# S5 scan of a Hyena/S5 diffusion trunk: groups of channels paired on the 128 rows, turns and lag matrices laid out in DRAM beforehand

## The chip, the cores and the metric

The kernel runs on one core of a Trainium2 chip. The metric is the device time of one execution in microseconds (us), lower is better. All data are float32; most large products are three-pass products of rounded halves, the products of the S5 stage are plain float32.

## The reference, cut to what matters

The program is one denoising step of a trunk of two layers over 1024 latent and 256 context tokens of width 1024: Hyena mixer, SwiGLU, S5 mixer, SwiGLU, final norm. The change concerns the S5 mixer: 64 groups of 16 channels, 64 complex states each, scanned forward and backward.

```python
def _s5_scan(ug, ab_re, ab_im, bb_re, bb_im, init):
    bu_re = jnp.einsum('blgh,gph->blgp', ug, bb_re)
    bu_im = jnp.einsum('blgh,gph->blgp', ug, bb_im)
    ...
    pr, pi, hr, hi = lax.associative_scan(_cmul_combine, (a_re, a_im, bu_re, bu_im), axis=1)
    if init is not None:
        hr = hr + pr * h0r - pi * h0i
        hi = hi + pr * h0i + pi * h0r
    return hr, hi

def _s5_mixer(u, j, p, h0):
    y = uf * p['s5_D'][j]
    for d in range(2):
        src = ug if d == 0 else jnp.flip(ug, axis=1)
        hr, hi = _s5_scan(src, ab_re, ab_im, bb_re, bb_im, init)
        yd = einsum('ghp,blgp->blgh', C_re, hr) - einsum('ghp,blgp->blgh', C_im, hi)
        ...
        y = y + yd
        if h0 is None:
            finals.append(jnp.stack([hr[:, -1], hi[:, -1]], axis=1))
    y = jax.nn.gelu(y)
    a, g = jnp.split(y @ p['s5_glu_w'][j] + p['s5_glu_b'][j], 2, axis=-1)
    return a * jax.nn.sigmoid(g), fin
```

## The kernel before, in words

The stages follow each other: filters, Hyena projection, Hyena core, Hyena output, the first SwiGLU, the S5 stage, its gate (GLU), the second SwiGLU, the final norm. Two pieces of S5 preparation are coroutines run beside other stages. `s5_tables` runs beside the Hyena projection: it makes the turn factors `W` by repeated complex products (`cmul`, L1015 to L1020) and stores them as `K.rot` (L1177). `s5_matrices` runs beside the first SwiGLU: it makes the entering matrices `K.tin`, the leaving matrices `K.wout` (L1239) and the lag blocks `K.kd` (L1252). `S5Scan.begin` is called in the last step of that SwiGLU, and `S5Scan.run` is the S5 stage.

The tokens are cut into chunks of 8 steps, so a group has WG = 162 columns: a zero column, 128 latent chunks, another zero column, and 32 context chunks. The 64 groups are taken in 8 pieces `k` of 8 groups. A tile of states has 128 rows, 64 states of the forward direction over 64 of the backward one, and 8 x 162 = 1296 columns.

For one piece: `norm` makes the modulated input `h` (on VectorE at L1328, for pieces 4, 5 and 6 on GpSimd at L1326; ScalarE adds the bias at L1330) and eight DMAs from ScalarE's queue spread it over rows as `u` (L1333). `enter` multiplies `u` by `ti` (16 matmuls of 162 columns, L1352) into six PSUM tiles, and VectorE turns these by `T` (L1353 to L1356, twelve operations). `T` holds 128 columns per group from DRAM (L1293, two DMAs); its 32 context columns are copied by ScalarE (L1342, L1343). `entered` adds the crossed products on GpSimd (L1361, L1362) and ScalarE puts the cached state into the zero columns (L1364, L1365). `scan` fills the decay tile `D0` on ScalarE (L1372) and runs four scans on VectorE: forward on rows 0 to 63 (L1376), backward on rows 64 to 127 (L1377), each for the real and the imaginary part, with 1296 columns. ScalarE saves the final states (L1378, L1379). The result is turned back: two products on GpSimd (`c`, `d`, L1383, L1384), two on VectorE (L1385, L1386). `scanned` subtracts `c` on VectorE (L1389). `leave` loads `wo` and, by eight DMAs from `K.kd`, the lag matrices `it`; 32 matmuls (L1405) add four terms into three PSUM tiles, ScalarE applies gelu (L1408) and stores (L1409).

The loop over `k` runs, in this order, enter(k), scanned(k-2), entered(k), leave(k-2), scan(k-1), norm(k+2). It only gives the program order; a planning scheduler with modelled costs sets the final order on each engine, and each engine runs its own list strictly in that order.

Of the kernel before, what the change touches and what calls it, by code (L numbers as in the profile page):

```python
# [1022 lines left out]
def s5_tables(K, io):  # L1023
# [13 lines left out]
    with ExitStack() as c:  # L1037
# [99 lines left out]
        for k in range(8):  # L1137
# [30 lines left out]
            W = bp.tile([128, 2, 8, 128], F32, tag="W", name="W")  # L1168
            t = [bp.tile([128, 8, 32], F32, tag=f"t{i}", name="t") for i in range(2)]
            V.tensor_copy(out=W[:, :, :, 0], in_=b0[:, :, g])  # L1170
            for i in range(7):
                n = 1 << i
                for a in range(0, n, 32):
                    e = min(n, 32)
                    cmul(V, pair(W[:, :, :, n + a:n + a + e]), pair(W[:, :, :, a:a + e]),
                         pair(pu[:, i, :, g].unsqueeze(3).to_broadcast([128, 2, 8, e])), [x[:, :, :e] for x in t])
            nc.sync.dma_start(out=K.rot[k], in_=W)  # L1177
# [3 lines left out]
def s5_matrices(K, io, p):  # L1181

    nc = K.nc
# [26 lines left out]
    for q in range(16):  # L1210
# [28 lines left out]
        nc.sync.dma_start(out=K.wout[k][:, :, e * 4:e * 4 + 4], in_=To.rearrange("p r g j h -> p r g (j h)"))  # L1239
# [20 lines left out]

class S5Scan:

# [4 lines left out]
    def begin(self, c):  # L1267
# [6 lines left out]
        self.z = z = zp.tile([128, 2, 8 * WG + 2], F32, name="Z")  # L1274
        self.D0 = zp.tile([128, 8, WG], F32, name="D0")
        for t in T:
            V.memset(t[:, :, :, 0:130:129], 0.0)
        for k in range(3):
            self.turn(k)
        V.memset(z[0:64, :, 0:2], 0.0)  # L1280
        V.memset(z[64:128, :, 8 * WG:8 * WG + 2], 0.0)
        V.memset(self.D0[:, :, 0:130:129], 0.0)
        self.fin = zp.tile([128, 2, 64], F32, name="fin")
        self.hin = zp.tile([128, 2, 64], F32, name="hin")
        self.q = [zp.tile([128, 2, 64], F32, name=f"q{i}") for i in range(2)]
# [3 lines left out]
        cmul(V, pair(self.hin), pair(self.q[0]), pair(K.u8), self.tiny)  # L1289

    def turn(self, k):
        for ri in range(2):
            self.K.nc.sync.dma_start(out=self.T[k % 3][:, ri, :, 1:129], in_=self.K.rot[k][:, ri])  # L1293

    def run(self, outs):
# [8 lines left out]
        with ExitStack() as c:  # L1304
            tp = c.enter_context(tc.tile_pool(name="st", bufs=6, reuse_waits="tile"))
            up = c.enter_context(tc.tile_pool(name="su", bufs=3, reuse_waits="tile"))
            U, R, AB, CD, DU = {}, {}, {}, {}, {}
# [4 lines left out]
            def norm(k):  # L1312
# [19 lines left out]
                for j in range(8):  # L1332
                    DU[k] = S_.dma_start(out=u[j * 16:j * 16 + 16], in_=h[:, j])  # L1333

            def enter(k):
# [6 lines left out]
                S_.copy(t[0:64, :, :, 130:162], t[0:64, :, :, 1:33])  # L1342
                S_.copy(t[64:128, :, :, 130:162], t[64:128, :, :, 97:129])  # L1343
# [15 lines left out]
            def entered(k):  # L1359
# [3 lines left out]
                g = slice(k * 8, k * 8 + 8)  # L1363
# [365 lines left out]
```

## Time and profile before

| | |
|---|---|
| median of 3 runs | 3635.53 us (3634.86 to 3645.38) |
| profiled execution, its own time | 3644.13 us |
| its span, first to last instruction | 3642.4 us |
| TensorE busy | 3308.8 us, 91% of the span |
| VectorE busy | 2371.9 us, 65% |
| ScalarE busy | 967.2 us, 27% |
| GpSimd busy | 688.5 us, 19% |
| mean granted TensorE clock | 0.953 of full speed |

The shares are means over stages with different limits, and the S5 stage is 7% of the span. In the profile's names PE is TensorE, DVE VectorE, ACT ScalarE, POOL GpSimd, SP the queue of SyncE; PEld is TensorE's weight load; a q behind an engine (ACTq) is its DMA issue.

### The profile page before, as it was taken

Reading aid. Unit: us, or ns where it says so; the run is one execution under the profiler, and the core shown is the slowest. Engines: PE = TensorE matmul, PEld = TensorE weight load, DVE = VectorE, ACT = ScalarE, POOL = GpSimd, SP = SyncE. Lnnn points to the kernel's source line nnn. Section 1 sums busy time; section 2 is a strip of 40 time slices with the busy share of each in tenths; the row PEclk is TensorE's granted clock in tenths of the full one; section 3 lists DMA queues with packets and bytes.
Section 4 is the critical chain, followed back from the end, with each engine's and each line's share of the span. In section 5 each row is a group of like instructions: output and inputs, shape, how many; then the busy total and the mean of one; then the engine's idle time right before and its main releaser. Section 6 shows DMA issues by size and latency. Waiting matters only on the chain. (4 is left out here: it accounts for less than half of the span.)

```text
span 3642.4 us, 48098 instructions
## 1 busy us (share of the span) xinstructions
PE 3308.8 (91%) x19078; PEld 2834.9 (78%) x19078; DVE 2371.9 (65%) x3910; ACT 967.2 (27%) x1674; POOL 688.5 (19%) x670
## 2 busy tenths in 40 slices
PE   5899699998869999999999994559999999999997
PEld 3788588887757788888888884547878888888886
DVE  5888988869994655655665558994255454554546
ACT  3555433332224411111111131213151111111112
POOL 1212300000022344333341014740120000000002
PEclk8999799999979999999999997779999999999998
DMA  7776353465436122121111125734101111111101
GB/s 229 242 254 204 120 179 127 151 221 199 148 127 202 38 68 70 64 70 64 64 62 54 41 57 136 168 87 128 47 24 42 40 35 41 35 45 37 35 30 58
DMA packets 292439, 368.21 MB, mean 101 GB/s; under 512 B 38415, under 2 KB 230615, under 8 KB 283256
## 3 DMA queue, kind: packets, MB, share of 16 engines
q1 hardware_dynamic: 278392, 343.53, 29.2%
q10 hardware_dynamic: 11520, 11.15, 1.4%
q0 software_dynamic: 2304, 10.49, 0.9%
q8 instruction: 150, 2.46, 0.3%
q14 instruction: 73, 0.60, 0.1%
HBM read 268.49 MB, written 91.29 MB: 99 GB/s over the span
## 5 line engine op out<-in xcount | busy, mean ns | idle before, releaser
L36 PE MATMUL ps<-hh,hi 128*128 128x512 f32 (+1 forms) x2688 | 952.7, 358 | 14.2 <-ACT hh L225 10.3
L37 PE MATMUL ps<-hl,hi 128*128 128x512 f32 (+1 forms) x2688 | 957.9, 357 | 8.3 <-POOL hl L96 5.7
L38 PE MATMUL ps<-hh,lo 128*128 128x512 f32 (+1 forms) x2688 | 953.1, 355 | 0.0
L184 DVE SCALAR_TENSOR_TENSOR x<-ps,mod,x 128x512 f32<-128x512 f32 (+1 forms) x1056 | 629.9, 653 | 11.6 <-PE ps L38 11.6
L36 PEld LDWEIGHTS ps<-hh,hi 128*128 128x128 f32 x2688 | 506.5, 189 | 94.9 <-ACT hh L225 11.6
L167 DVE TENSOR_TENSOR nw<-nw,ps 128x512 f32<-128x512 f32 x132 | 78.8, 597 | 766.4 <-PE ps L38 760.9
L37 PEld LDWEIGHTS ps<-hl,hi 128*128 128x128 f32 x2688 | 508.9, 189 | 86.8 <-POOL hl L96 11.7
L38 PEld LDWEIGHTS ps<-hh,lo 128*128 128x128 f32 x2688 | 507.6, 189 | 73.6 <-issue 0.5
L37 PE MATMUL ps<-gl,hi 128*128 128x512 f32 (+1 forms) x1056 | 375.3, 355 | 0.0
L36 PE MATMUL ps<-gh,hi 128*128 128x512 f32 (+1 forms) x1056 | 373.4, 355 | 1.2 <-DVE x L184 1.2
L38 PE MATMUL ps<-gh,lo 128*128 128x512 f32 (+1 forms) x1056 | 374.2, 354 | 0.0
L57 POOL TENSOR_TENSOR st<-st,sq 128x512 f32<-128x512 f32 (+1 forms) x72 | 92.2, 1283 | 1180.2 <-ACT sq L56 1177.7
L32 DVE TENSOR_TENSOR lo<-raw,hi 128x1024 fp32r<-128x1024 f32 x156 | 207.0, 1327 | 94.9 <-ACT hi L31 94.6
L31 ACT CAST hi<-raw 128x1024 fp32r<-128x1024 f32 x156 | 163.6, 1049 | 350.9 <-PE ps L37 320.1
L36 PEld LDWEIGHTS ps<-gh,hi 128*128 128x128 f32 x1056 | 198.8, 188 | 32.0 <-DVE x L184 2.1
L37 PEld LDWEIGHTS ps<-gl,hi 128*128 128x128 f32 x1056 | 199.0, 188 | 29.4 <-issue 1.2
L38 PEld LDWEIGHTS ps<-gh,lo 128*128 128x128 f32 x1056 | 199.0, 188 | 28.8 <-issue 0.7
L36 PE MATMUL ps<-hh,wh 128*128 128x512 f32 (+1 forms) x576 | 210.3, 366 | 11.5 <-ACT hh L95 11.5
L37 PE MATMUL ps<-hl,wh 128*128 128x512 f32 (+1 forms) x576 | 208.6, 363 | 7.9 <-DVE hl L92 6.2
L38 PE MATMUL ps<-hh,wl 128*128 128x512 f32 (+1 forms) x576 | 207.5, 362 | 0.0
L170 ACT CAST gh<-nw 128x512 fp32r<-128x512 f32 x132 | 72.2, 547 | 483.7 <-DVE nw L167 483.7
L166 ACT ACTIVATE nw<-ps 128x512 f32<-128x512 f32 x132 | 69.3, 525 | 490.8 <-PE ps L38 489.7
(364 smaller groups left out, 5294.8 us busy)
## 6 DMA issues: line engine op xcount, KB each, us to landing
adaw<-in_ada_w SPq DMA_DIRECT2D x96, 512.0 KB, 5.0
raw<-in_w13p SPq DMA_DIRECT2D x88, 512.0 KB, 3.6
raw<-in_w2p SPq DMA_DIRECT2D x44, 512.0 KB, 3.2
kspec<-KO SPq DMA_DIRECT2D x16, 1024.0 KB, 5.1
K<-kspec SPq DMA_DIRECT2D x16, 1024.0 KB, 5.7
raw<-in_hy_inp SPq DMA_DIRECT2D x24, 512.0 KB, 3.3
rot<-W SPq DMA_DIRECT2D x8, 1024.0 KB, 6.9
tin<-tst SPq DMA_DIRECT2D x32, 256.0 KB, 2.7
```

Source lines behind the costliest of these rows:

```text
L31: K.nc.scalar.copy(hi, raw)
L32: K.nc.vector.tensor_tensor(out=lo, in0=raw, in1=hi.bitcast(F32), op=ALU.subtract)
L36: nc.tensor.matmul(ps, wh, xh, start=first, stop=False, **kw)
L37: nc.tensor.matmul(ps, wh, xl, start=False, stop=False, **kw)
L38: nc.tensor.matmul(ps, wl, xh, start=False, stop=last, **kw)
L57: nc.gpsimd.tensor_tensor(out=st, in0=st, in1=sq, op=ALU.add)
L166: nc.scalar.activation(out=sa, in_=ps[0], func=AF.Silu)
L167: nc.vector.tensor_tensor(out=sa, in0=sa, in1=ps[1], op=ALU.mult)
L170: nc.scalar.copy(gh, sa)
L184: K.nc.vector.scalar_tensor_tensor(out=x, in0=p, scalar=self.G(d, COND[tb]), in1=x, op0=ALU.mult, op1=ALU.add)
```

## The change

A tile of states still has 128 rows, but they are now 2 groups x 64 states, and the direction lies along the columns: 2 directions x 4 pairs of groups x 162. So one scan covers a direction of all 8 groups on 128 rows with 648 columns. What follows from this, and what is moved besides:

- `W` has 162 columns. GpSimd zeroes two of them, ScalarE copies the context columns (two copies per piece, in `s5_tables`), and four DMAs store it regrouped; `T` is then one DMA, and its memsets and copies in the S5 stage are gone.
- `K.wout` is stored regrouped by four DMAs instead of one. `K.it` is new: eight DMAs from DRAM to DRAM per piece, at the end of its part of `s5_matrices`; `it` is then one load instead of eight.
- Enter: 32 matmuls on 64 array columns each instead of 16. Leave: the `it` term stays whole (8 matmuls), the other three terms become 48 matmuls on 64 array rows each; two groups that run on the two row halves write different banks, so four PSUM tiles are held instead of three, and gelu comes in four pieces.
- The cached state goes in by two GpSimd copies after the adds, the final state out by two VectorE copies after the scans (both ScalarE before). Decay, cached state and final state are regrouped by 4, 8 and 8 small DMAs.
- The eight `u` DMAs alternate between ScalarE's and SyncE's queue, and the first `it` load no longer is held behind them.

```diff
-            W = bp.tile([128, 2, 8, 128], F32, tag="W", name="W")
+            W = bp.tile([128, 2, 8, WG], F32, tag="W", name="W")
+            P.memset(W[:, :, :, 0:130:129], 0.0)
...
-            nc.sync.dma_start(out=K.rot[k], in_=W)
+            nc.scalar.copy(W[0:64, :, :, 130:162], W[0:64, :, :, 1:33])
+            nc.scalar.copy(W[64:128, :, :, 130:162], W[64:128, :, :, 97:129])
+            for d in range(2):
+                for i in range(2):
+                    nc.sync.dma_start(out=K.rot[k][i * 64:i * 64 + 64, :, d], in_=W[d * 64:d * 64 + 64, :, i::2])
...
+        if e:
+            for j in range(8):
+                nc.sync.dma_start(out=K.it[k, j * 16:j * 16 + 16], in_=K.kd[k * 8:k * 8 + 8, :, 7 - j:15 - j, :].rearrange("g h s x -> h g (s x)"))
...
-                    DU[k] = S_.dma_start(out=u[j * 16:j * 16 + 16], in_=h[:, j])
+                    (S_, nc.sync)[j % 2].dma_start(out=u[j * 16:j * 16 + 16], in_=h[:, j])
...
-                            nc.tensor.matmul(ps[ri][:, i], ti[:, g0 + i, ri], u[:, g0 + i], start=True, stop=True)
+                            d, pr = divmod(g0 + i, 4)
+                            for e in range(2):
+                                rows = slice(e * 64, e * 64 + 64)
+                                nc.tensor.matmul(ps[ri][rows, i], ti[:, 2 * pr + e, ri, d * 64:d * 64 + 64], u[:, 2 * pr + e],
+                                                 start=True, stop=True, tile_position=(0, e * 64))
...
-                S_.copy(r[0:64, :, :, 0], hin[0:64, :, g])
-                S_.copy(r[64:128, :, :, 129], hin[64:128, :, g])
+                g = slice(k * 4, k * 4 + 4)
+                P.tensor_copy(out=r[:, :, 0:4, 0], in_=hin[:, :, 0, g])
+                P.tensor_copy(out=r[:, :, 4:8, 129], in_=hin[:, :, 1, g])
...
-                    V.tensor_tensor_scan(out=z[0:64, ri, 2:N + 2], data0=d[0:64], data1=x[0:64], initial=0.0, op0=MUL, op1=ADD)
-                    V.tensor_tensor_scan(out=z[64:128, ri, 0:N][:, ::-1], data0=d[64:128, ::-1], data1=x[64:128, ::-1], initial=0.0, op0=MUL, op1=ADD)
-                S_.copy(fin[0:64, :, g], z[0:64, :, 1 + WG:2 + N:WG])
-                S_.copy(fin[64:128, :, g], z[64:128, :, 130:N:WG])
+                    V.tensor_tensor_scan(out=z[:, ri, 0, 2:N + 2], data0=d[:, 0], data1=x[:, 0], initial=0.0, op0=MUL, op1=ADD)
+                    V.tensor_tensor_scan(out=z[:, ri, 1, N - 1::-1], data0=d[:, 1, ::-1], data1=x[:, 1, ::-1], initial=0.0, op0=MUL, op1=ADD)
+                V.tensor_copy(out=fin[:, :, 0, g], in_=z[:, :, 0, WG + 1:N + 2:WG])
+                V.tensor_copy(out=fin[:, :, 1, g], in_=z[:, :, 1, 130:N:WG])
...
-                        nc.tensor.matmul(ps[gl // 3][:, gl % 3], w[:, gl], x[:, gl], start=(i == gl % 3 == 0), stop=(i == 3 and gl in (2, 5, 7)))
+                    for d in range(2):
+                        for gl in range(8):
+                            rows = slice(gl % 2 * 64, gl % 2 * 64 + 64)
+                            nc.tensor.matmul(at(gl), w[rows, d, gl // 2], x[rows, d * 4 + gl // 2], start=False,
+                                             stop=(i == 2 and d == 1 and gl >= 4), tile_position=(gl % 2 * 64, 0))
```

The operations on GpSimd between two scans stand in another order. Before, around the turning of piece 1 and the adds of piece 3 (`h_20083` is piece 4's input, `R_20108` belongs to piece 3):

```order
L1383 TENSOR_TENSOR c_20077<-Z_19602,T1_19600 128x1296
L1384 TENSOR_TENSOR d_20078<-Z_19602,T1_19600 128x1296
L1315 MEMSET h_20083 128x8x2
L1326 TENSOR_TENSOR h_20083<-x0_10285,st0_105 128x128x2 x2
L1326 TENSOR_TENSOR h_20083<-x1_10286,st1_106 128x128x2 x2
L1326 TENSOR_TENSOR h_20083<-x2_10287,st2_107 128x32x4 x2
L1362 TENSOR_TENSOR R_20108<-R_20108,b_20110 128x1296
L1361 TENSOR_TENSOR R_20108<-R_20108,a_20109 128x1296
```

In the change, from the adds of one piece (`R_20172`) to the copies of the cached state into it:

```order
L1389 TENSOR_TENSOR R_20172<-R_20172,b_20174 128x1296
L1388 TENSOR_TENSOR R_20172<-R_20172,a_20173 128x1296
L1411 TENSOR_TENSOR c_20307<-Z_19763,T1_19761 128x1296
L1412 TENSOR_TENSOR d_20308<-Z_19763,T1_19761 128x1296
L1340 MEMSET h_20313 128x8x2
L1351 TENSOR_TENSOR h_20313<-x0_10334,st0_106 128x128x2 x2
L1351 TENSOR_TENSOR h_20313<-x1_10335,st1_107 128x128x2 x2
L1351 TENSOR_TENSOR h_20313<-x2_10336,st2_108 128x32x4 x2
L1391 COPY R_20172<-hin_19777 128x2x4
L1392 COPY R_20172<-hin_19777 128x2x4
```

The two copies are new on this engine, and they stand not right behind their adds but behind the previous piece's two products and the next input's six; the scans of `R_20172` read what they write.

On TensorE, one leave before (`ps_20423` to `ps_20425` are its three PSUM tiles) begins:

```order
L1405 MATMUL ps_20423<-u_19964,it_20414 128x162 x3
L1405 MATMUL ps_20424<-u_19964,it_20414 128x162 x3
L1405 MATMUL ps_20425<-u_19964,it_20414 128x162 x2
L1405 MATMUL ps_20423<-R_20108,wo_20412 128x162 x3
L1405 MATMUL ps_20424<-R_20108,wo_20412 128x162 x3
```

And in the change, where `ps_20560` and `ps_20561` hold the groups of array rows 0 to 63 and `ps_20562` and `ps_20563` those of rows 64 to 127, with the enter before it:

```order
L1378 MATMUL ps_20537<-u_20323,ti_20495 64x162 x4
L1378 MATMUL ps_20538<-u_20323,ti_20495 64x162 x4
L1429 MATMUL ps_20560<-u_20069,it_20558 128x162 x3
L1429 MATMUL ps_20561<-u_20069,it_20558 128x162
L1429 MATMUL ps_20562<-u_20069,it_20558 128x162 x3
L1435 MATMUL ps_20560<-R_20172,wo_20556 128x162
L1435 MATMUL ps_20562<-R_20172,wo_20556 128x162
L1435 MATMUL ps_20560<-R_20172,wo_20556 128x162
L1435 MATMUL ps_20562<-R_20172,wo_20556 128x162
```

Per piece the instructions go from 16 + 32 to 32 + 8 + 48, and the last kind alternates between the two row halves.

## Rows read from the trace of the kernel before

**Rows 1.** Busy time by engine in three stretches: the S5 stage from its first turn on, then its tail.

```profile
core 0: us, PE busy (x) PEld busy (x) DVE busy (x) ACT busy (x) POOL busy (x), PEclk, DMA share, GB/s
2204.90:2220.20 15.30, 9.70 (x58) 9.46 (x57) 14.91 (x30) 2.00 (x4) 6.04 (x3) 0.83 0.92 210
2220.20:2453.70 233.50, 123.04 (x677) 119.51 (x678) 229.95 (x144) 41.90 (x86) 139.68 (x53) 0.74 0.49 124
2453.70:2465.40 11.70, 4.16 (x30) 3.91 (x28) 3.54 (x9) 4.45 (x8) 0.00 (x0) 0.79 0.81 257
```

**Rows 2.** Groups by line and form, 2204 to 2465 us (line, engine, operation, count | busy, mean ns | idle before).

```profile
L1376 DVE TENSOR_TENSOR_SCAN Z<-D,R 64x1296 f32<-64x1296 f32 x16 | 67.0, 4200 | 2.7 <-ACT R L1364 2.6
L1377 DVE TENSOR_TENSOR_SCAN Z<-D,R 64x1296 f32<-64x1296 f32 x16 | 50.6, 3172 | 0.3
...
L1384 POOL TENSOR_TENSOR d<-Z,T 128x1296 f32<-128x1296 f32 x8 | 32.0, 3997 | 14.6 <-DVE Z L1377 14.6
L1362 POOL TENSOR_TENSOR R<-R,b 128x1296 f32<-128x1296 f32 x8 | 28.5, 3560 | 47.8 <-DVE R L1355 47.8
L1383 POOL TENSOR_TENSOR c<-Z,T 128x1296 f32<-128x1296 f32 x8 | 27.3, 3414 | 54.7 <-DVE Z L1377 31.9 <-issue 22.8
...
L1364 ACT COPY R<-hin 64x16 f32<-64x16 f32 x8 | 1.8, 220 | 25.8 <-POOL R L1361 22.5 <-issue 2.8 <-ACT u L1408 0.4
```

**Rows 3.** Timeline of VectorE, single instructions (start, duration).

```profile
2218.04 0.66 DVE L1356 TENSOR_TENSOR a<-ps,T 128x486 f32<-128x486 f32 x1
2218.61 0.49 DVE L1353 TENSOR_TENSOR R<-ps,T 128x324 f32<-128x324 f32 x1
...
2220.22 10.82 DVE L1376 TENSOR_TENSOR_SCAN Z<-D,R 64x1296 f32<-64x1296 f32 x2
...
2244.72 2.65 DVE L1328 SCALAR_TENSOR_TENSOR h<-x,an,st 128x256 f32<-128x256 f32 x6
...
2261.21 2.85 DVE L1377 TENSOR_TENSOR_SCAN Z<-D,R 64x1296 f32<-64x1296 f32 x1
...
2269.86 1.51 DVE L1385 TENSOR_TENSOR R<-Z,T 128x1296 f32<-128x1296 f32 x1
2271.28 0.66 DVE L1353 TENSOR_TENSOR R<-ps,T 128x486 f32<-128x486 f32 x1
```

**Rows 4.** Timeline of GpSimd beside it.

```profile
2216.70 2.93 POOL L1361 TENSOR_TENSOR R<-R,a 128x1296 f32<-128x1296 f32 x1
...
2222.85 5.48 POOL L1361 TENSOR_TENSOR R<-R,a 128x1296 f32<-128x1296 f32 x1
2236.81 2.48 POOL L1383 TENSOR_TENSOR c<-Z,T 128x1296 f32<-128x1296 f32 x1 [8.48 <-issue]
...
2243.37 0.12 POOL L1315 MEMSET h<- 128x16 f32 x1
...
2327.60 6.11 POOL L1326 TENSOR_TENSOR h<-x,st 128x256 f32<-128x256 f32 x6
```

**Rows 5.** Timeline of TensorE: products on 32 array columns in the first SwiGLU, two leaves.

```profile
1301.89 0.65 PE L1245 MATMUL ps<-To,bbd 128*32 128x128 f32 x16
1302.47 0.39 PE L36 MATMUL ps<-hh,hi 128*128 128x256 f32 x1
...
2248.31 2.28 PE L1405 MATMUL ps<-d,wo 128*128 128x162 f32 x12
...
2448.03 4.66 PE L1405 MATMUL ps<-R,wo 128*128 128x162 f32 x16 [6.82 <-ACT u L1408]
```

**Rows 6.** Busy time by engine beside which the tables and the matrices are made.

```profile
484.00:760.00 276.00, 275.62 (x1497) 237.96 (x1496) 209.50 (x642) 100.77 (x147) 10.26 (x10) 1.00 0.45 153
1270.00:1960.00 690.00, 690.00 (x3824) 584.80 (x3823) 400.27 (x644) 121.55 (x192) 271.99 (x385) 1.00 0.20 66
```

**Rows 7.** Timeline of the start of the S5 stage.

```profile
2195.08 10.40 ACTq L1333 DMA_DIRECT2D u<-h  x16
...
2204.91 0.67 DVE L1353 TENSOR_TENSOR R<-ps,T 128x486 f32<-128x486 f32 x1 [9.87 <-PE ps L1352]
```

More of the change, by code (lines that the diff above doesn't have):

```diff
@@ L1238, in s5_matrices @@
         spread(To, pout, C, Cn)
-        nc.sync.dma_start(out=K.wout[k][:, :, e * 4:e * 4 + 4], in_=To.rearrange("p r g j h -> p r g (j h)"))
+        for d in range(2):
+            for i in range(2):
+                nc.sync.dma_start(out=K.wout[k][i * 64:i * 64 + 64, :, d, e * 2:e * 2 + 2],
+                                  in_=To[d * 64:d * 64 + 64, :, i::2].rearrange("p r g j h -> p r g (j h)"))
         yield
@@ L1252, in s5_matrices, with swap_halves @@
                 nc.sync.dma_start(out=K.kd[q * 4 + i, :, s:s + 7].rearrange("h s x -> h (s x)"), in_=kd[r:r + 16, j * 16:j * 16 + 112])
+        if e:
+            for j in range(8):
+                nc.sync.dma_start(out=K.it[k, j * 16:j * 16 + 16], in_=K.kd[k * 8:k * 8 + 8, :, 7 - j:15 - j, :].rearrange("g h s x -> h g (s x)"))
 WG = 162
 NORM_POOL = (4, 5, 6)
+def swap_halves(nc, out, x, back=False):
+    for d in range(2):
+        for i in range(2):
+            ds, is_ = slice(d * 64, d * 64 + 64), slice(i * 64, i * 64 + 64)
+            if back:
+                nc.sync.dma_start(out=out[ds, i::2], in_=x[is_, d])
+            else:
+                nc.sync.dma_start(out=out[is_, d], in_=x[ds, i::2])
 class S5Scan:
@@ L1380, in scan @@
[L1380 to L1386 removed]
+                    x = halves(r[:, ri])
+                    V.tensor_tensor_scan(out=z[:, ri, 0, 2:N + 2], data0=d[:, 0], data1=x[:, 0], initial=0.0, op0=MUL, op1=ADD)
@@ new lines, in scan @@
+                    V.tensor_tensor_scan(out=z[:, ri, 1, N - 1::-1], data0=d[:, 1, ::-1], data1=x[:, 1, ::-1], initial=0.0, op0=MUL, op1=ADD)
+                V.tensor_copy(out=fin[:, :, 0, g], in_=z[:, :, 0, WG + 1:N + 2:WG])
+                V.tensor_copy(out=fin[:, :, 1, g], in_=z[:, :, 1, 130:N:WG])
+                zr, zi = (z[:, ri, :, 1:N + 1] for ri in range(2))
+                CD[k] = a, b = tmp("c"), tmp("d")
+                tr, ti = halves(t[:, 0]), halves(t[:, 1])
+                P.tensor_tensor(out=halves(a), in0=zi, in1=ti, op=MUL)
@@ L1388, in scanned @@
+                P.tensor_tensor(out=halves(b), in0=zr, in1=ti, op=MUL)
+                V.tensor_tensor(out=halves(r[:, 0]), in0=zr, in1=tr, op=MUL)
+                V.tensor_tensor(out=halves(r[:, 1]), in0=zi, in1=tr, op=MUL)
             def scanned(k):
@@ L1392, in leave @@
                 u, r, (a, b) = U.pop(k), R.pop(k), CD.pop(k)
-                wo = up.tile([128, 2, 8, 128], F32, tag="w", name="wo")
+                wo = up.tile([128, 2, 2, 4, 128], F32, tag="w", name="wo")
                 nc.sync.dma_start(out=wo, in_=K.wout[k])
                 it = up.tile([128, 8, 128], F32, tag="it", name="it", bufs=1)
-                with ExitStack() as late:
-                    if k == 0:
-                        late.enter_context(tc.issue_after(DU[1].ins))
-                    for j in range(8):
-                        (nc.sync if k else S_).dma_start(out=it[j * 16:j * 16 + 16], in_=K.kd[k * 8:k * 8 + 8, :, 7 - j:15 - j, :].rearrange("g h s x -> h g (s x)"))
@@ L1401, in leave @@
[L1401 to L1408 removed]
+                nc.sync.dma_start(out=it, in_=K.it[k])
@@ L1409, in leave @@
+                for e in range(2):
+                    S_.activation(out=u[:, e:e + 5:2], in_=ps[e][0], func=AF.Gelu_apprx_tanh)
+                    S_.activation(out=u[:, e + 6], in_=ps[e][1][:, 0], func=AF.Gelu_apprx_tanh)
                 S_.dma_start(out=K.yg[k].rearrange("j (h g) c -> (j h) (g c)", g=8), in_=fl(u))
@@ L1425, in run @@
                     norm(k + 2)
-            cmul(V, pair(q[1]), pair(fin), pair(K.w31), tiny)
+            for ri in range(2):
+                swap_halves(nc, q[2][:, ri], fin[:, ri], back=True)
+            cmul(V, pair(q[1]), pair(q[2]), pair(K.w31), tiny)
             nc.sync.dma_start(out=outs["state"], in_=q[1])
```

65 lines of the change are left out of this document (29 added, 36 removed).

## The prediction, made before the changed kernel ran

> **What bounds the kernel now.** First the engines' shares: TensorE is busy 91% of the span. That holds for the long products and says nothing of the S5 stage, where the change lies, so I read the stretches next [rows 1]. From 2204.9 to 2453.7 us, 248.8 us, VectorE is busy 244.9 us, TensorE 132.7 us, GpSimd 145.7 us. The stage lasts as long as VectorE's list. The groups by line [rows 2] say what fills the list: the scans, 32 instructions and 117.6 us, with means of 4200 and 3172 ns. The timeline [rows 3] shows that a scan with nothing beside it takes 2.85 us; two others, started at 2220.22, took 10.82 us. In those same microseconds a GpSimd add, alone 2.93 us, took 5.48 us [rows 4]. So operations with two operands in SBUF run one after the other, whichever of the two engines they are on: the long ones contain the other engine's turn. VectorE's operations from PSUM are not held up so: 0.66 us at 2218.04 while GpSimd's add of 2216.70 ran [rows 3, 4].
>
> That gives a model of the stage, one piece of eight: four scans of 2.85 us (11.4); GpSimd's four products or adds, three of 2.93 and one of 2.48 us (11.3); three VectorE operations of 1.42 us, the distance between the starts at 2269.86 and 2271.28 (4.3) [rows 3, 4]; the norm, on GpSimd for three pieces (6.11 us each, 2.3 per piece as a mean), on VectorE for three others in this stretch (2.65 us, 1.0 per piece). Sum 30.3 us, times 8 is 242 us, against 248.8 us measured. The twelve enter operations of a piece (8 of 486 columns, 0.57 us from start to start at 2218.04, and 4 of 324, 0.49 us less the same overlap, 0.40: 6.2 us) lie beside GpSimd's work.
>
> **The change, part by part.** The sum is made against the profiled execution, 3644.1 us, which is 8.6 us above the median of the runs, 3635.5 us.
>
> *Scans.* Eight groups of one direction on 128 rows and 648 columns in place of 64 rows and 1296: as many instructions, half the columns. The enter operations show what does not halve: 486 columns take 0.66 us, 324 take 0.49 us [rows 3], so 0.17 us per 162 columns, and about 0.15 us of a duration is fixed; the next start hides part of that. A scan then costs 1.43 us (half) to 1.50 us; I take 1.46. Saved: 4 x 1.39 x 8 = 44.5 us, all on the path, since nothing else than these exclusive operations sets the stage.
>
> *State copies.* Two GpSimd copies per piece of 128 x 8 elements: the nearest row on that engine is a memset of 128 x 16, 0.12 us [rows 4]. Two VectorE copies: the nearest is ScalarE's 0.22 us [rows 2]. I take 0.3 us per piece on the path, 2.5 us in all, between 0 (all beside PSUM work) and 5.5 us (all of it). The ScalarE copies that go were off the path. Ceiling of the gain: 44.5 - 2.5 = 42 us.
>
> *Cover and queues.* Before, GpSimd stood idle 117 us waiting mostly for scans or for the enter of the next piece (47.8 + 54.7 + 14.6 [rows 2]). These pauses absorbed every delay of TensorE, DMA or ScalarE; shorter scans halve them. And the copies of the cached state now stand on GpSimd's list behind the previous piece's two products and, for three pieces, behind the six norm operations as well. The scans of a piece wait for them. If all of this is exposed it costs three times 6.11 us, 18 us; if VectorE has enters or turning to do meanwhile, nothing. I take 10 us, the middle, since neither end has a row nearer to it.
>
> *Enter on TensorE.* 16 matmuls become 32 on half of the array's columns. A float32 matmul leaves two records (763 of them for the stage's 8 x 48 matmuls [rows 1]). A row bears on whether two such halves run together: 16 records on 32 array columns, 128 moving columns each, took 0.65 us, 0.04 us apiece, while the 12 records of whole matmuls at 2248.31 took 2.28 us, 0.19 apiece for 162 columns [rows 5]. For 128 columns that would be 0.15. So column tiles ran together there, and I take 32 halves to last as long as 16 whole ones. The Trainium skill, "TensorE: Matmul & The Clock Gate", Part 3, states that weight loads overlap running matmuls only where the row group differs, and these halves share all rows; by that rule the 32 would go one by one. The row speaks against it, on narrower tiles than these.
>
> *Leave on TensorE.* 8 whole and 48 half-row matmuls. Where two alternate between row halves, as they mostly do, the 48 take the time of 24, and the leave costs what its 32 did. A change of the tile form shows no gap: the tiles of 1301.89 end by the model at 1302.54, and the next whole matmul starts at 1302.47 [rows 5]. Taken as 0. At most it is the 0.58 us between those two starts, three times a piece, 14 us of TensorE time, of which the stage leaves 116 us idle [rows 1]. A leave also holds four PSUM tiles instead of three, so with the enter's six a piece asks for 10 where it asked for 9; what waits come of it are in the 10 us above.
>
> *Tail and start.* After the last scan the last leave stands alone on the path: more issues, four gelus instead of three and the final state's eight DMAs before the output. I add 2 us to the 11.7 us that the tail has [rows 1], bounds -2 and +4. At the start, 16 `u` issues on one queue took 10.4 us, 0.65 each, and VectorE sat idle 9.87 us for the first product [rows 7]. With half on SyncE's queue the first piece is issued 2.6 us sooner, if the 8 new loads of the cached state, which stand ahead on that queue, are issued by then. Bounds -2.6 and +3; I take 0. The Trainium skill, "DMA: Bandwidth & Descriptors", Rules for kernel authors, says that issuing from several engines saves issue time only; by it the split is worth those 2.6 us at most.
>
> *Preparation.* In `s5_tables` the copies and three more stores per piece stand beside a TensorE that is busy 275.6 of 276.0 us, with VectorE at 209.5 [rows 6]: 66 us of slack cover a longer wait for the buffer of `W`. In `s5_matrices` (690.0 of 690.0 us) the 64 new DMAs and the split stores are on SyncE's queue, past the weight loads; nothing computed waits. Both 0, upper bound 3 us together. The first turn's loads get shorter, the T copies go from ScalarE; both off the path.
>
> Sum: -42 + 10 + 2 = **-30 us**: 3614 us by the profiled execution, 3606 us by the median.
>
> **The rivals.**
> 1. *Full cover* (0.13). Nothing is given back: the full 42 to 45 us, 3591 to 3594 us. For it: 6.2 us of enters against 13.8 us of GpSimd work per piece. Against: the halved pauses.
> 2. *GpSimd's list takes the scan's place* (0.20). The state copies behind norms and products cost all 18 us, and the halved pauses up to 16 more: 42 less 20 to 34, a gain of 8 to 22 us, 3614 to 3628 us. For it: the order shown above. Against: VectorE has turns to do meanwhile.
> 3. *TensorE becomes the bound*, slower (0.10). The half-tile matmuls go one by one. Then a piece has 88 matmuls, 176 records, instead of 48 and 96. At 0.179 us per record (136.9 us of TensorE over the 763 records [rows 1]) that is 31.5 us a piece, 252 us for the stage. Beside that TensorE must stand still at the first and the last scans and turns (each 4 x 1.46 + 2.93 + 1.42, 10 us) and until the gate's input is there (some 6 us of the tail): 278 us against the 260.5 us of rows 1, +17 us, 3653 us. It decides from about 0.167 us per record on, where 1408 records and 26 us fill 260.5 us; at 0.29 us, as the 16 records of 2448.03 took [rows 5], it would cost far more. For it: TensorE's work in records nearly doubles. Against: 0.04 us apiece at 1301.89 [rows 5]. [...]
> 4. *The scans do not shorten* (0.07). If a scan's time went with elements over all rows, the change leaves the list as it is: 3636 to 3640 us. Against: 128-row operations of 1296 columns take 1.42 us [rows 3], so the doubled rows cost nothing in VectorE's other operations.
>
> **How the numbers follow.** The forecast, a gain of 22 to 38 us, has 0.50, rival 1 0.13, rival 2 0.20, rival 3 0.10, rival 4 0.07. About 0.3% (11 us) is what a measurement of this kernel can tell from no change. Faster by more: 0.50 + 0.13 + 0.15 of rival 2 = 0.78. Within: 0.05 of rival 2 and 0.05 of rival 4, 0.10. Slower: rival 3 and the rest of rival 4, 0.12. The range leaves out rivals 3 and 4: from full cover with a shorter start (3588) to rival 2's end (3628).
>
> **What would show it.** Right: 32 scans of 128 x 648 with a mean near 2 us or less and 1.5 where nothing is beside them; the stretch that was 248.8 us about 219; VectorE still over 90% busy in it; half-tile matmuls that start under 0.1 us apart; windows of the tables and matrices as long as before. Wrong: scans that wait for a GpSimd copy of the cached state (rival 2), VectorE idle for TensorE's products with matmul starts 0.15 us or more apart (rival 3), scans still of 2.8 us (rival 4).

## The result, and the profile after

The changed kernel takes 3664.1 us (median of 5, 3652.7 to 3667.8) against 3638.7 us of the kernel before in the same comparison: ratio 1.0068, interval 1.0054 to 1.0082. It is slower by 0.7%, where 30 us less were forecast, and lies outside the range. The profiled execution took 3660.2 us, span 3658.4 us, 16.0 us more than before; the medians are 25 us apart, since the execution profiled before lies 5 us above its median here and the one after 4 us below. The rows below place the 16 us.

The end points of the stages tell where the time went. The first and last start of the ScalarE operation L706 frame the Hyena projection. From the last norm factor (L82) to the first turn runs the start of the S5 stage, from there to the last store of `yg` the stage itself. All are rows of the timeline or of a line's view. The rows that are shown nowhere else, first before, then after the change (last norm factor, last subtraction of `c` on VectorE, last store):

```profile
2193.34 0.43 DVE L82 SCALAR_TENSOR_TENSOR st<-nw,st 128x256 f32<-128x256 f32 x1
...
2452.22 1.50 DVE L1389 TENSOR_TENSOR R<-R,c 128x1296 f32<-128x1296 f32 x1
...
2458.34 0.38 ACTq L1409 DMA_DIRECT2D yg<-u  x1
```

```profile
2221.91 0.42 DVE L82 SCALAR_TENSOR_TENSOR st<-nw,st 128x256 f32<-128x256 f32 x1
...
2451.18 4.00 DVE L1417 TENSOR_TENSOR R<-R,c 128x1296 f32<-128x1296 f32 x1
...
2473.07 0.33 ACTq L1440 DMA_DIRECT2D yg<-u  x1
```

In us:

| | first L706 | projection | start of S5 | S5 stage | from last `yg` store to the end | span |
|---|---|---|---|---|---|---|
| before | 375.0 | 387.2 | 11.6 | 253.4 | 1184.1 | 3642.4 |
| after | 369.1 | 422.4 | 24.2 | 227.0 | 1185.3 | 3658.4 |

So +35.2, +12.6, -26.4 and +1.2 us; the other -6.6 us is nearly all in front of the projection, where nothing was changed (its start lies between 360.8 and 375.0 us in all the runs below). **The S5 stage as a whole gained nearly what was forecast; two stages that I had put down at nothing took it back and more.** Inside the S5 stage the parts came out otherwise: from the first turn to the end of the last subtraction 248.8 us became 209.1, and from there to the last store 4.6 us became 17.9.

The projection stage, by its waits in the changed kernel (engine, line, what it waited for: us, times, longest):

```profile
POOL W L1169 <- DMA rot<-W: 112.9, 7, 30.6
...
DVE W L1171 <- DMA rot<-W: 36.7, 7, 7.0
...
PE ps L687 <- DVE y L675: 27.9, 5, 8.5
```

The same waits before, with one issue of the store:

```profile
DVE W L1170 <- DMA rot<-W: 11.6, 3, 4.0
...
PE ps L687 <- DVE W L1017: 0.3, 1, 0.3
...
556.37 0.33 SPq L1177 DMA_DIRECT2D rot<-W  x1
```

TensorE is now busy 248 of 276 us where it was 275.6 [rows 6]:

```profile
484.00:760.00 276.00, 248.13 (x1310) 213.40 (x1309) 191.24 (x598) 96.62 (x144) 10.07 (x15) 0.96 0.50 129
```

Over the whole projection, before and after (the first number behind the comma is TensorE's busy time, the third from the end its mean granted clock):

```profile
375.00:762.20 387.20, 358.34 (x1896) 307.40 (x1895) 315.20 (x931) 146.65 (x224) 34.31 (x29) 0.95 0.45 152
```

```profile
369.10:791.50 422.40, 365.53 (x1896) 312.90 (x1895) 316.42 (x933) 154.99 (x239) 37.01 (x37) 0.93 0.51 144
```

So of the 35.2 us TensorE stood idle for 28.0, and for 7.2 it was busy longer with the same 1896 records, at a lower mean granted clock. From 490 to 550 us, busy 59.4 of 60, TensorE had a clock of 1.00; from 550 to 610, with pauses and busy 45.6, it had 0.91.

One release of `W` in the timeline, from its last product to the next piece's first copy:

```profile
552.47 0.42 DVE L1020 TENSOR_TENSOR W<-t 128x256 f32<-128x256 f32 x1
...
552.93 0.64 ACT L1179 COPY W<-W 64x512 f32<-64x512 f32 x1 [5.79 <-DVE W L1020]
552.96 4.48 SPq L1182 DMA_DIRECT2D rot<-W  x4
...
564.86 0.20 DVE L1171 COPY W<-b 128x16 f32<-128x16 f32 x1 [7.04 <-DMA rot<-W]
564.94 1.93 DVE L675 SCALAR_TENSOR_TENSOR y<-z,scw,y 128x128 f32<-128x128 f32 x4
```

Four issues of 4.5 us together, where one took 0.33 us, and a landing put `W` out of use for 12 us. The copy into `W` stands on VectorE's list in front of L675, the short convolution whose result TensorE transposes at L687.

The start of the S5 stage (issues on SyncE's and ScalarE's queue, then VectorE's first turn) answers to [rows 7]. Before, the entering matrices had left here, 13 us ahead of the last norm factor:

```profile
2180.41 1.28 SPq L1338 DMA_DIRECT2D ti<-tin  x3
```

After:

```profile
2216.27 9.94 SPq L1280 DMA_DIRECT2D hin<-q  x8
...
2223.70 18.64 ACTq L1358 DMA_DIRECT2D u<-h  x8
2226.32 2.27 SPq L1363 DMA_DIRECT2D ti<-tin  x3
2228.69 15.86 SPq L1358 DMA_DIRECT2D u<-h  x8
...
2246.10 0.67 DVE L1380 TENSOR_TENSOR R<-ps,T 128x486 f32<-128x486 f32 x1 [22.50 <-PE ps L1378]
```

A `u` issue took 2.3 and 2.0 us, not 0.65. Packets under 512 B went from 38,415 to 80,848 over the span: the swap DMAs take every second element of a row, so they move pieces of 4 bytes, 2048 per DMA and 40,960 in the twenty of decay, cached and final state.

In the S5 stage the groups by line answer to [rows 2]:

```profile
L1412 POOL TENSOR_TENSOR d<-Z,T 128x1296 f32<-128x1296 f32 x8 | 29.7, 3707 | 0.0
...
L1404 DVE TENSOR_TENSOR_SCAN Z<-D,R 128x648 f32<-128x648 f32 x16 | 26.8, 1714 | 23.8 <-POOL R L1391 23.8
...
L1405 DVE TENSOR_TENSOR_SCAN Z<-D,R 128x648 f32<-128x648 f32 x16 | 23.0, 1480 | 0.0
L1407 DVE COPY fin<-Z 128x8 f32<-128x8 f32 x8 | 17.9, 2233 | 0.0
...
L1391 POOL COPY R<-hin 128x8 f32<-128x8 f32 x8 | 3.0, 377 | 0.3
```

The scans take 49.8 us where they took 117.6. They wait 23.8 us for the copy of the cached state, in fact for what GpSimd does ahead of it, since the copy itself takes 0.2 us as a median. The second of the two final-state copies, of 8 columns, takes 2.2 us as a mean; such a copy takes 0.14 us by itself, and 2.72 us beside GpSimd's product:

```profile
2275.39 4.03 POOL L1412 TENSOR_TENSOR d<-Z,T 128x1296 f32<-128x1296 f32 x1
2276.79 2.72 DVE L1407 COPY fin<-Z 128x8 f32<-128x8 f32 x1
...
2298.64 0.14 DVE L1406 COPY fin<-Z 128x8 f32<-128x8 f32 x1
```

And the end of the stage:

```profile
2445.87 7.07 SPq L1278 DMA_DIRECT2D q<-fin  x6
...
2453.03 0.94 SPq L1424 DMA_DIRECT2D it<-it  x1
...
2460.62 4.41 PE L1429 MATMUL ps<-u,it 128*128 128x162 f32 x16 [11.82 <-DMA it<-it]
```

The last leave waits for its lag matrices, whose load stands on SyncE's queue behind six swaps of the final state.

TensorE did not become the bound: the column tiles of an enter and the row tiles of a leave both leave a record every 0.07 us, against 0.15 us for the whole matmuls of a leave, all three at a granted clock of 1.00. (The 0.19 us at 2248.31 [rows 5] was at 0.79.) The second line is the window view of the enter's time, with the busy time of TensorE, then of its weight loads.

```profile
2302.74 4.62 PE L1378 MATMUL ps<-u,ti 128*64 128x162 f32 x64
...
2302.70:2307.30 4.60, 4.60 (x66) 4.33 (x65) 4.60 (x3) 0.86 (x3) 4.60 (x4) 1.00 0.02 4
...
2439.75 2.23 PE L1429 MATMUL ps<-u,it 128*128 128x162 f32 x15
...
2469.48 2.37 PE L1435 MATMUL ps<-R,wo 64*128 64x162 f32 x32
```

### The profile page after: what moved, and what is told of

Same layout as the page of the kernel before. It is cut to its first block, busy times and chain, and to the rows that moved or that the text cites. A ratio compares the mean times of both kernels' runs of the same rounds, so it can differ in the third digit from the quotient of the medians.

```text
span 3658.4 us, 49577 instructions
## 1 busy us (share of the span) xinstructions
PE 3338.9 (91%) x19718; PEld 2853.1 (78%) x19718; DVE 2306.9 (63%) x3923; ACT 957.3 (26%) x1650; POOL 671.0 (18%) x694
## 2 busy tenths in 40 slices
DMA packets 348193, 377.16 MB, mean 103 GB/s; under 512 B 80848, under 2 KB 289432, under 8 KB 339001
## 4 chain that ended last, share of the span: by engine, by line
PE 71%; DVE 16%; DMA 6%; issue 2%; POOL 2%; ACT 1%; SPq 1%; ACTq 0%; DVEq 0%; POOLq 0%
PE ps L36 22%; PE ps L37 22%; PE ps L38 22%; DVE E L807 4%; DVE AB L807 2%; DMA rot<-W 1%; PE acc L872 1%; PE ps L270 1%; DMA adaw<-in_ada_w 1%; DVE y L675 1%; DVE nw L89 1%; PE ps L687 1%; DMA yr<-yv 1%; PE ps L1435 1%; DVE Z L1404 0%
## 5 line engine op out<-in xcount | busy, mean ns | idle before, releaser
L36 PE MATMUL ps<-hh,wh 128*128 128x512 f32 (+1 forms) x576 | 212.0, 369 | 12.8 <-ACT hh L95 12.8
```

Source lines behind the costliest of these rows:

```text
L36: nc.tensor.matmul(ps, wh, xh, start=first, stop=False, **kw)
```

## The experiments

Ratios are to the kernel before, in the same comparison, with 95% intervals; the changed kernel's is 1.0068. The time in front of the projection alone differs by up to 14 us between the profiles, so a small gain is read from the rows of the stage that was changed.

**The table W: a second buffer, fewer pieces, undone, and alone.**

```diff
-            W = bp.tile([128, 2, 8, WG], F32, tag="W", name="W")
+            W = bp.tile([128, 2, 8, WG], F32, tag="W", name="W", bufs=2)
```

> The changed kernel with two buffers for the table tile W instead of one. Theory A: the 29 us lost beside the Hyena projection are VectorE standing behind its copy into W until the four stores of the last W have landed (36.7 us of such waits); with a second buffer these waits fall below 5 us, the projection stage is back within 3 us of the kernel before, and the run is 25 to 29 us faster than the changed kernel, near 3635. Rival B: what costs is SyncE's queue, where four stores of 512 pieces take 4.5 to 5.4 us to issue and hold the weight loads; then a second buffer gains under 8 us, and the weight loads or stores show up as what TensorE waits for.

Ratio 1.0031 (1.0018 to 1.0044), 3647.2 us; projection 410.4 us. A third of the projection's loss came back. The planner used the second buffer to place the copies into `W` earlier on VectorE's list, and there they wait again:

```profile
DVE W L1171 <- DMA rot<-W: 28.8, 5, 6.2
```

So the waits did not fall as theory A had it, and a queue (rival B) was not ruled out by this run. Fewer and longer pieces in the store:

```diff
-                    nc.sync.dma_start(out=K.rot[k][i * 64:i * 64 + 64, :, d], in_=W[d * 64:d * 64 + 64, :, i::2])
+                    nc.sync.dma_start(out=K.rot[k][i * 64:i * 64 + 64, :, d], in_=W[d * 64:d * 64 + 64, :, i * 4:i * 4 + 4])
```

(with the powers that fill `W` copied into the same order of groups)

> The changed kernel with the groups of W already in the order of the target, so that the four stores have 128 pieces of 2592 bytes each instead of 512 of 648; still one buffer, still the memset and the two copies in the chain. Theory A: the chain from the last product of W to its release is copies, four issues and a landing; issues fall from about 1.2 to 0.4 us each and the landing by 1 to 2 us, so of the 29 us about a half to two thirds come back, 13 to 20 us. Rival B: if the pieces on the queue are all of it, 25 us or more come back; if the added copies and memset are what counts, under 8 us.

Ratio 1.0007 (0.9997 to 1.0017), 3638.9 us; projection 405.3 us, so 17 of 35 us back. The four issues still take 3.9 to 5.1 us; the landing fell from 8.2 to 5.2 us. The pieces are about half of it. VectorE's waits for the store are then nearly what they were before the change, yet TensorE still waits 10.8 us at L687, now for products of `W` that stand in front of L675:

```profile
DVE W L1173 <- DMA rot<-W: 12.2, 6, 2.9
...
PE ps L687 <- DVE W L1017: 5.2, 2, 2.8
```

So the wait for the buffer is not all of it; what makes the rest of the table part's cost stays open. The table part undone:

```diff
-            W = bp.tile([128, 2, 8, WG], F32, tag="W", name="W")
+            W = bp.tile([128, 2, 8, 128], F32, tag="W", name="W")
...
-            for d in range(2):
-                for i in range(2):
-                    nc.sync.dma_start(out=K.rot[k][i * 64:i * 64 + 64, :, d], in_=W[d * 64:d * 64 + 64, :, i::2])
+            nc.sync.dma_start(out=K.rot[k], in_=W)
...
+                    self.K.nc.sync.dma_start(out=self.T[k % 3][i * 64:i * 64 + 64, ri, d * 4:d * 4 + 4, 1:129], in_=self.K.rot[k][d * 64:d * 64 + 64, ri, i::2])
...
+                S_.copy(t[:, :, 0:4, 130:162], t[:, :, 0:4, 1:33])
+                S_.copy(t[:, :, 4:8, 130:162], t[:, :, 4:8, 97:129])
```

> The changed kernel with the table part undone: W has 128 columns again and one store, the turn is put in order by eight loads of 512-byte runs and two ScalarE copies per piece in the S5 stage. Theory A: everything lost beside the Hyena projection is W's longer chain from last product to release; a second buffer gave back only part because VectorE's list then asked for the buffer earlier and still waited 28 us. So the projection is as long as before (within 3 us), and the run is 22 to 30 us faster than the changed kernel; the S5 stage is up to 4 us longer for the eight loads. Rival B: part of the loss comes from other things on SyncE's queue; then 8 us or more of the 29 stay.

Ratio 0.998 (0.997 to 0.9989), 3628.2 us, by the ratios 32 us under the changed kernel. The projection is 386.5 us, as before; the whole loss there is the table part. The S5 stage is 229.1 us. The start grew to 30.0 us: the swaps left with the last norm factor (2185.86 against 2185.74 us) and not 5.6 us ahead of it, took 15.8 us to issue, and half of `u` stood behind them.

The same part alone on the kernel before, with the turn loaded back into the old order of rows:

> The kernel before with the table part of the change alone: W with its zero and context columns made beside the Hyena projection and stored by four DMAs, the turn loaded by four DMAs back into the old order of rows. Theory A: the projection stage is 20 to 30 us longer and the S5 stage within 3 us, so 18 to 30 us slower than the kernel before. Rival B: the loss needs the changed kernel's other loads on the queue: under 8 us slower.

Ratio 1.0075 (1.0054 to 1.0097), 3661.6 us, 26 us slower. L706 in its line view (count: shortest, median and longest in ns, first and last start), then in that of the kernel before, of the changed kernel, and of the table part undone:

```profile
L706 ACT ACTIVATE z<-ps,hyinb x72: 457/687/691, 368.2 to 785.7; 128x512 f32<-128x512 f32 x48, 128x256 f32<-128x256 f32 x24
```

```profile
L706 ACT ACTIVATE z<-ps,hyinb x72: 455/688/692, 375.0 to 762.2; 128x512 f32<-128x512 f32 x48, 128x256 f32<-128x256 f32 x24
```

```profile
L706 ACT ACTIVATE z<-ps,hyinb x72: 452/687/691, 369.1 to 791.5; 128x512 f32<-128x512 f32 x48, 128x256 f32<-128x256 f32 x24
```

```profile
L706 ACT ACTIVATE z<-ps,hyinb x72: 455/688/693, 369.6 to 756.1; 128x512 f32<-128x512 f32 x48, 128x256 f32<-128x256 f32 x24
```

First to last start: 417.5, 387.2, 422.4 and 386.5 us. The table part costs the projection 30 to 36 us, added and taken away, as theory A has it. Without the turn's copies the S5 stage of the run on the kernel before fell by 5.8 us to 247.7, more than the 3 us that theory A allowed; the table part saves that and costs five times as much.

**The swaps, and what stands behind them.** Runs of 128 bytes:

```diff
-                nc.sync.dma_start(out=out[is_, d], in_=x[ds, i::2])
+                nc.sync.dma_start(out=out[is_, d], in_=x[ds, i])
```

(the small products before and after write and read the sorted order)

> The changed kernel, with decay, cached state and final state put in the order of the target before the small swap DMAs, so that each of their rows is one run of 128 bytes instead of 32 pieces of 4 bytes. Theory A: the 4-byte pieces are what holds the queues: the eight loads of the cached state issue in about 3 us instead of 9.9, the sixteen u issues take 0.65 us each instead of about 2, the first product starts 10 to 13 us earlier after the norm, the last lag load no longer holds the last leave (5 to 9 us), and the run is 15 to 22 us faster than the changed kernel. Rival C: the split of the u loads over two queues slows their issue; then the u issues stay near 2 us each and the run gains under 6 us.

Ratio 1.0017 (1.0007 to 1.0026), 3641.5 us: about 18 us back, as expected, but the rows place only 11.6 of them in what was changed: start 17.0 us (7.2 less, where 10 to 13 were expected), S5 stage 222.6 (4.4 less). The rest lies mostly in and before the projection, where this edit changes nothing. The eight loads take 4.9 us, but the `u` issues still 1.7 us each:

```profile
2208.15 4.93 SPq L1280 DMA_DIRECT2D hin<-q  x8
2213.20 1.47 SPq L1367 DMA_DIRECT2D ti<-tin  x3
2215.27 13.70 SPq L1362 DMA_DIRECT2D u<-h  x8
```

With the second buffer of `W` as well:

> Both edits of the two runs before together. Theory A: the gains lie in different stages and add, 40 to 50 us under the changed kernel, 3614 to 3624, which is 14 to 25 us under the kernel before; what is left of the prediction is then the S5 stage's own gain of about 30 us. If the S5 stage's gain were only the other side of a loss elsewhere (rival B), the sum stays above 3630.

Ratio 0.9996 (0.9986 to 1.0006), 3633.3 us; short of the expected sum, mostly by what the second buffer fell short. The time lies above 3630 as rival B said, but not for its reason: projection 409.1, start 17.0, S5 stage 223.4 us. The edits add, each in its stage, and the S5 stage keeps its 30 us.

Two attempts at the other 5 us of the start failed. First, the entering matrices issued ahead of the swaps:

```diff
+                last = nc.sync.dma_start(out=ti, in_=K.tin[k])
...
+                behind.enter_context(tc.issue_after(last.ins))
```

> The changed kernel with the first three loads of the entering matrices (3 MB) issued ahead of the eight swap DMAs of the cached state, which themselves stay as they are, in pieces of 4 bytes. Theory A, in two parts: of the 12 us lost at the start some 7 are the 4-byte pieces and some 5 the late loads of the entering matrices, which share the DMA engines with u; so this edit alone brings 3 to 6 us. Rival C: the pieces are all of it, and ahead of u as before they hold it up as long: under 2 us.

Ratio 1.0063 (1.0047 to 1.008), start 32.4 us. The edit did not do what it was to do: the loads, moved up in the queue, still left only with the last norm factor (2210.87 against 2210.38 us), and the swaps behind 3 MB then took 22.5 us to issue, in front of half of `u`. Second, `u` on one queue:

```diff
-                    (S_, nc.sync)[j % 2].dma_start(out=u[j * 16:j * 16 + 16], in_=h[:, j])
+                    S_.dma_start(out=u[j * 16:j * 16 + 16], in_=h[:, j])
```

> The changed kernel with all u loads on ScalarE's queue again. Theory A: half of the first u loads stand on SyncE's queue behind the eight swap DMAs of the cached state and the 3 MB of entering matrices, and that is most of the 12 us lost at the start; on ScalarE's queue alone they take about 10 us from the norm on, so the first turn starts 8 to 12 us earlier and the run is 6 to 12 us faster than the changed kernel, near 3654. Rival C: the 4-byte pieces in flight hold the DMA engines for every queue; then the u loads take 15 us or more on ScalarE's queue too, and under 4 us come back.

Ratio 1.004 (1.0028 to 1.0051), but the start is 22.9 us and the sixteen issues take 22.8: rival C's row. The 10 us in the time I can't place; the first L706 of its profile starts 7 us earlier, which no edit explains.

Combinations on top of the table part undone and runs of 128 bytes:

> The changed kernel with the table part undone, the swaps in runs of 128 bytes and the entering matrices loaded first. Theory A: projection stage as before, start as before within 2 us, S5 stage 28 to 32 us shorter than before: 3604 to 3612, 24 to 32 us under the kernel before. Rival: the u loads split over two queues and the four-tile leave keep the start or the tail 5 us or more longer, 3615 and over.

Ratio 0.9938 (0.9923 to 0.9953), 3613.6 us, just above the expected range; S5 stage 223.9 us, but the start is 23.8 us where it was to be as before: what the rival said of the start.

> The changed kernel with the table part undone, the swaps in runs of 128 bytes, all u loads on ScalarE's queue, the swaps ahead of the entering matrices as in the change. Theory A: start within 4 us of the kernel before's 11.6 us (from the last norm factor to the first turn), S5 stage about 224 us against 253: 3600 to 3608. Rival: the loads share the DMA engines and the start stays at 17 us or more, as with the split: 3610 and over.

Ratio 0.9936 (0.9916 to 0.9957), 3611.5 us, start 21.7 us: the rival.

> As the run before, with the three entering matrices loaded ahead of the swaps. Theory A: they are then through the queue before u starts, so the start is 1 to 5 us shorter than in the run before; the swaps come behind 3 MB and take some 14 us, but nothing needs the cached state before the first scans. Rival: u shares the DMA engines with them either way: within 2 us of the run before.

Ratio 0.9934 (0.9915 to 0.9953), 3611.2 us, start 19.8 us. In none of the three did the start come back; in each the 3 MB of entering matrices left within 6 us of the last norm factor, beside `u`. In the kernel before they left 13 us ahead of it. So the next runs put that to the test. The swaps alone on the kernel before, into a spare tile:

```diff
+        spare = zp.tile([128, 2, 2, 32], F32, name="spare")
+        for ri in range(2):
+            swap_halves(nc, spare[:, ri], self.hin[:, ri])
```

> The kernel before, with eight swap DMAs in pieces of 4 bytes added behind the product of the cached state, into a spare tile that nothing reads; the loads of the entering matrices stand behind them on SyncE's queue. Theory A: these loads are then issued beside u and not 13 us before the last norm factor, and the pieces hold the queues: the start grows from 11.6 to 20 us or more, the run is 8 to 12 us slower than the kernel before. Rival C: the start is longer in the change for something else (the u split, the turn's load); then the start stays within 3 us of 11.6.

Ratio 1.0031 (1.0018 to 1.0043), 3645.2 us, 9 us slower; start 23.1 us, with every other part of the change absent. The pieces and the late matrices come together in this run, which does not tell them apart:

```profile
2175.95 9.33 SPq L1269 DMA_DIRECT2D spare<-hin  x8
2185.39 3.14 SPq L1352 DMA_DIRECT2D ti<-tin  x3
...
2183.86 22.21 ACTq L1347 DMA_DIRECT2D u<-h  x16
```

And, on the run with ratio 0.9936, the swaps off that queue, on GpSimd's (those of the final state too):

```diff
-            swap_halves(nc, self.hin[:, ri], q2[:, ri])
+            swap_halves(nc, self.hin[:, ri], q2[:, ri], eng=nc.gpsimd)
...
+                swap_halves(nc, self.q2[:, ri], fin[:, ri], back=True, eng=nc.gpsimd)
```

> Table part undone, swaps in runs of 128 bytes and issued by GpSimd, u on ScalarE's queue. Theory A: with nothing ahead of them the entering matrices are loaded 10 us or more before the last norm factor, u has the DMA engines to itself, and the start is within 2 us of the kernel before's 11.6 us, some 8 to 10 us shorter than with the swaps on SyncE's queue: 3600 to 3606. Rival: the start stays at 18 us or more.

Ratio 0.9908 (0.9893 to 0.9923), 3601.4 us. Start 12.9 us:

```profile
2176.93 1.28 SPq L1367 DMA_DIRECT2D ti<-tin  x3
...
2189.03 4.20 POOL L1275 DMA_DIRECT2D hin<-q  x8 [5.98 <-issue]
...
2190.32 10.41 ACTq L1362 DMA_DIRECT2D u<-h  x16
```

The swaps still run beside `u`, and each `u` issue takes 0.65 us again: what came back, 9 us, goes with the entering matrices, which left 11 us ahead of the last norm factor (2188.37 us). The final state's swaps left SyncE's queue too, and the S5 stage fell to 213.8 us, 10 to 12 us under the runs above. Against the run with ratio 0.9936, 6 of them lie behind the last subtraction: TensorE's wait for the last lag load, 8.1 us there, is gone. The other 5 lie in front of it, and their cause stays open.

> As the run before with the u loads split over ScalarE's and SyncE's queues as in the change. Theory A: with nothing in front on SyncE's queue the first piece's eight loads are issued in half the time; the start is 0 to 3 us shorter than in the run before. Rival: the DMA engines are the limit, the sixteen loads take as long on two queues as on one: within 1 us.

Ratio 0.9916 (0.9901 to 0.993), 3604.1 us, start 12.8 us: within 1 us, the rival. The split of `u` is worth nothing here.

**The small state copies.** Both back on ScalarE, against the run with ratio 0.9938:

```diff
-                P.tensor_copy(out=r[:, :, 0:4, 0], in_=hin[:, :, 0, g])
+                S_.copy(r[:, :, 0:4, 0], hin[:, :, 0, g])
...
-                V.tensor_copy(out=fin[:, :, 0, g], in_=z[:, :, 0, WG + 1:N + 2:WG])
+                S_.copy(fin[:, :, 0, g], z[:, :, 0, WG + 1:N + 2:WG])
```

(and their second lines)

> As the run before, with the small copies of cached and final state back on ScalarE. Theory A: on GpSimd they make the scans wait (23.8 us of waits for the cached-state copy in the changed kernel), and on VectorE the second final-state copy takes 2.2 us as a mean because it waits for GpSimd's products; taken off both, the S5 stage is 4 to 12 us shorter. Rival D: the scans wait for the adds ahead of these copies, not for the copies, and VectorE waits for GpSimd at the next operation anyway: within 3 us of the run before.

Ratio 0.9968 (0.9957 to 0.998), 3622.8 us, 9 us slower: neither theory. The S5 stage grew from 223.9 to 232.5 us, VectorE's wait for the cached state from 25.1 to 39.4 us:

```profile
DVE Z L1410 <- ACT R L1397: 39.4, 5, 14.3
```

The final-state copies alone on ScalarE, against the run with ratio 0.9908:

> As the run with the swaps on GpSimd's queue and u on ScalarE's, with the copies of the final state on ScalarE and those of the cached state still on GpSimd. If the copies of the cached state made the 9 us (ScalarE has gelu, bias and u issues in its list ahead of them, and the scans wait for them), this run is within 3 us of that one; if those of the final state did (gelu and the decay fill stand behind them on ScalarE while they wait for the scans), it is 5 to 9 us slower.

Ratio 0.9888 (0.9873 to 0.9903), 3594.0 us, **42 us under the kernel before and the best of all**; S5 stage 208.6 against 213.8 us. That is faster than either expectation allowed: the final-state copies are better on ScalarE, where one takes 0.2 us. So the loss with both on ScalarE should be the cached state's; that copy was not moved by itself. The two intervals overlap, but no run of the one is as slow as any of the other (3591.4 to 3595.9 against 3596.6 to 3604.3 us). The copies had filled 28.3 us of VectorE's list, of which only these 5 came back.

## Why the prediction was wrong

- *Scans: 1.46 us each, 44.5 us saved.* Right for the single scan: alone they last 1.48 us, 1.41 from start to start (two from 2311.77 to 2314.59). From the first turn to the last subtraction the best version is 44.8 us shorter than before (204.0 us against 248.8), but 15 us of waits for GpSimd are in it, so that the figure agrees is in part chance.
- *State copies, cover and queues: 2.5 + 10 us given back.* Less was: 39.7 of 44.5 us stayed, and the stretch that was to be about 219 us took 209. VectorE's busy time in the stretch fell by 66 us (scans 67.8 less, final-state copies 24.6 more, the rest from other operations) and its idle time grew by 26, so it is busy 86% and not over 90%. The scans do wait 23.8 us for GpSimd's copy of the cached state, the sign named for rival 2; on ScalarE they wait longer. The final-state copies, put at 0.2 us from a ScalarE row, cost 2.2 and 0.8 us on VectorE, where they wait for GpSimd's products as two-operand work does; some 5 us come back with them on ScalarE.
- *Tail: 2 us, bounds -2 and +4.* **Failed,** though the whole stage hid it: +13.3 us from the last subtraction to the last store. The final state's swaps were counted as work before the output, and they stood on SyncE's queue in front of the last lag load, for which TensorE waited 11.8 us. In the best version this end takes 4.6 us, as before. With the copies and the cover, 18 us were given back where 14.5 had been put down: near by luck, since one term was too large and the other too small.
- *Enter and leave on TensorE: no longer than before.* Right; the tiles run in pairs, and rival 3 fell. Its prices of 0.179 and 0.29 us per record came from stretches at granted clocks of 0.75 and 0.50. The rule of the Trainium skill on row groups ("TensorE: Matmul & The Clock Gate", Part 3) speaks of weight loads; that the column tiles would go one by one by it was the prediction's own step. This trace does not agree with either: 64 records in 4.62 us, and weight loads on the same rows busy 4.33 us of that time.
- *Preparation: 0, upper bound 3 us.* **The step that failed:** "66 us of slack cover a longer wait for the buffer of W". Slack was summed over a stage, but a wait on an engine with a fixed order holds what is queued behind it at that moment. Seven waits of 5 us in front of L675 became 28 us of TensorE waits and, with 7 us of the same matmuls at a lower granted clock, 35 us of stage. The trace of before already had the row that should have warned: VectorE waited three times, 11.6 us, for this very store. In all seven releases `W`'s next copy came 4.0 to 7.3 us after the issue of the store, so there was little slack to use; it now comes 11.0 to 13.3 us after the first issue. The longer wait is shown for about half of the loss, by the run with fewer pieces; that the table part is all of it is shown by taking it away and by adding it alone. I counted the added stores as issues and not as a longer release.
- *Start: 0, bounds -2.6 and +3.* **Failed too**, measured +12.6. I had asked whether the swaps "are issued by then" and not what they carry and what stands behind them. About 7 us are pieces of 4 bytes (24.2 to 17.0 us). Most of the other 5 go with the entering matrices, whose loads had left 13 us before the last norm factor and now left beside `u`; that share is what was left over, since the one edit that moved these loads alone did not bring them forward. The Trainium skill, "DMA: Bandwidth & Descriptors", Rules for kernel authors, says that issuing from several engines saves issue time only; the last comparison of the split agrees, 12.8 us of start against 12.9, so not even 2.6 us came of it.
- The rivals missed the loss, because all four were sought in the S5 stage. None said that a preparation step could set the time of the stage it runs beside.

## What to carry to other kernels

Work that is moved out of a tight stage into the shade of another has to be costed there on its engine's list: what is queued behind its waits, and whether the buffer it uses had any slack; a wait for that buffer in the trace before says no. Small DMAs are costed by their pieces and by what stands behind them on the queue, not by their bytes: in the change, twenty transfers of 8 KB and what they held up took back some 20 us, nearly half of what halving the scans gained. Where a rearrangement must be made, a run of 128 bytes or another engine's queue is cheaper than pieces of 4 bytes on the queue that feeds the path.

## What the runs showed of the hardware that was not expected

- A VectorE copy of 128 x 8 with one operand in SBUF took 0.14 us by itself and up to 2.74 us beside a GpSimd product: here a one-operand copy from SBUF waits for GpSimd too.
- Two 64-column tiles on the same array rows run at once: 0.072 us per record over 64 records, as fast as two 64-row tiles (0.074) and twice as fast as whole matmuls (0.149), all at a granted clock of 1.00.
- Issues stretch with the traffic ahead of them: eight swaps of 8 KB took 4.9 us in runs of 128 bytes and 14.4 behind 3 MB of loads; in pieces of 4 bytes they took 9.9 and 22.5.
